# Three large PSUM tiles, fp32r transposes behind a DMA copy, and projections chained to a stream

## The chip, the cores and the metric

One NeuronCore of a Trainium2 chip runs the whole program. Its engines are TensorE (PE in the profile, with PEld for its weight loads), VectorE (DVE), ScalarE (ACT), GpSimd (POOL) and SyncE (SP), which issues most DMAs. The metric is the device time of one execution in microseconds; lower is better.

## The reference

One encoder layer is applied to two groups with the same weights, a prompt of 1024 tokens and a sample of 512, in fp32. Its core:

```python
h = rms_norm(x, ln_pre)
z = h @ w_in                  # pool_in, pool_gate, q, k, v, attn_gate, xq, x_gate, merge_logits
pool_out = multiscale_pool(pool_in, w_pool, pool_scale)
q = apply_rope(rms_norm(q, q_norm), cos, sin);  k = apply_rope(rms_norm(k, k_norm), cos, sin)
attn_out = self_attention(q, k, v)              # softmax(q k^T) v, 8 heads of 64, 2 k/v heads
cross_out = cross_attention(xq, rms_norm(mem, ln_mem), w_mem_kv)   # 4 heads of 128, 256 memories
branches = (pool_out * silu(pool_gate), attn_out * silu(attn_gate), cross_out * silu(x_gate))
gates = sigmoid(merge_logits + b_merge)
merged = sum over n of gates[n] * (branches[n] @ w_branch[n])
return x + rms_norm(merged @ w_out, ln_post)
```

The model width is 1024, the input projection has 6400 columns, and everything is kept to fp32 accuracy.

## The kernel before

Matrices are multiplied in fp32r, a form of fp32 that the matmul takes in one pass. Each operand is split into a high part (a copy rounded to fp32r on ACT, `split`, L165) and a low part (the rest, on DVE, L162), and `mm3` (L126 through `mm`) adds high x high, high x low and low x high in PSUM. A transpose is a matmul with an identity: `tr` (L130) uses `ident` for fp32 tiles and `identr` for fp32r tiles.

PSUM is shared out in two kinds of tiles. `A()` is 128 x 1024 (two banks), and there are two of them; `B()` is 128 x 512 (one bank), and there are four. A tile's next user waits until the last reader of its earlier user is done. A scheduler orders the instructions of each engine by priority and puts in the waits; what an engine then does is fixed.

The program runs in these stages:

- the memories' keys and values (`mem_phase`), and the prompt group's normalised input (`long_h`);
- `products`, the prompt group's input projection. Two weight tiles of 128 columns and the two token blocks of 512 make a 2 x 2 block product, done with seven products in place of eight (25 pairs of weight tiles). The seven products accumulate in banks named by the letters of "XYXZXZX", each product being twelve matmuls of 512 columns. Some results are read between: `keep` (L358, ACT) copies a partial sum out, `summed` (L416, DVE, or L414, ACT) adds a kept one to a bank. Tails of finished projections (`kv_tail`, `q_tail`, `pool_tail`) come in between as background;
- `plain`, the sample group's projections: 24 matmuls for each weight tile into one B tile. Nine pairs are run by themselves, the other pairs become the fill of the next stage;
- the stream. Its units are 64 self-attention units of the prompt (`attention`), 8 cross-attention units (`cross`), 16 double units of the sample (`pairs_of`) and 4 cross units. A unit has four steps: `ahead` loads, `scores` computes scores into an A tile, the row maximum (L782 for the first 64) and the exponential (L784), whose probabilities POOL scales (L786); `turn` transposes them, eight 128 x 128 pieces into an A tile, and splits the result; `values` multiplies with v into a B tile and gates. `stream` runs, in iteration i, scores of unit i, turn of unit i - LAG and values of unit i - LAG - VLAG, and after each step `weave` lets as much of the fill run as the step's share allows;
- what is left of the fill, and then `branches(0)`: branch outputs are loaded from DRAM, split (L165), multiplied with `w_branch` into B tiles and merged with the gates (L996, L998);
- three `block` stages with the other branch projections, the output projection (`out_phase`, in A and B tiles), the norm and the stores.

Intermediate results (q, gates, branch outputs) go through scratch in DRAM, loaded and stored by SP.

## Time and profile before

| | us |
|---|---|
| median of 3 runs | 1500.23 |
| lowest run | 1493.72 |
| the profiled execution's own time | 1496.65 |
| span of that profile, first to last instruction | 1494.8 |
| PE busy | 1456.0 (97%) |
| DVE busy | 976.5 (65%) |
| ACT busy | 709.6 (47%) |
| POOL busy | 273.3 (18%) |
| DMA queue 1, share of 16 engines | 42.7% |

One of the three runs took 2429.65 us; the median leaves it out. In the profile's rows "out<-in" are tiles without their numbers, "xN" is how many instructions a row stands for, and what follows "<-" in brackets or behind a time is the instruction that ended a wait. Matmuls overlap, so their lengths (0.39 us for 512 columns) are longer than the step from one start to the next (0.23 us).

### The profile page before, as it was taken

The numbers are of one execution on the slowest core, as the hardware profiler recorded it, in microseconds if no ns is written. First come the engines' busy times: TensorE is split into PE (matmuls) and PEld (weight loads), VectorE is DVE, ScalarE is ACT, GpSimd is POOL, SyncE is SP. The second block draws the span as 40 slices with busy tenths as digits, with TensorE's granted clock in tenths as the row PEclk, the third lists the DMA queues.
The fourth block names the chain that finished last, engine by engine and source line by source line (L and its number), as shares of the span: only waits on it lengthen the run. The fifth ranks groups of instructions, "written<-read, shape, count | busy, mean of one in ns | idle before, by whom it ended". The sixth has DMA issues, their size and how long they took to land.

```text
span 1494.8 us, 19564 instructions
## 1 busy us (share of the span) xinstructions
PE 1456.0 (97%) x7264; PEld 1210.1 (81%) x7264; DVE 976.5 (65%) x1215; ACT 709.6 (47%) x1083; POOL 273.3 (18%) x286
## 2 busy tenths in 40 slices
PE   7979999999999999999999999999998999999998
PEld 5768888888888888887888888888886888888887
DVE  6996586666648564747767666676775664764764
ACT  6444444544434545434656556566675233323332
POOL 1000020110000000301222222234232150250241
PEclk9989999999999999999999999999999999999999
DMA  7513233332422434344222223165446844954952
GB/s 277 172 47 106 85 114 125 108 132 66 129 92 78 158 133 128 102 150 148 64 96 80 91 68 106 58 219 173 155 155 214 286 148 132 347 193 140 336 163 84
DMA packets 88174, 211.37 MB, mean 141 GB/s; under 512 B 9872, under 2 KB 19216, under 8 KB 87312
## 3 DMA queue, kind: packets, MB, share of 16 engines
q1 hardware_dynamic: 88080, 210.14, 42.7%
q8 instruction: 57, 0.93, 0.3%
q14 instruction: 37, 0.30, 0.1%
HBM read 155.57 MB, written 54.53 MB: 141 GB/s over the span
## 4 chain that ended last, share of the span: by engine, by line
PE 85%; DMA 4%; DVE 4%; ACT 4%; issue 2%; SPq 1%; POOL 0%; DVEq 0%; POOLq 0%; ACTq 0%
PE B L126 66%; PE A L126 14%; PE A L130 5%; ACT u L784 1%; DVE s L782 1%; ACT whi L165 1%; DMA raw<-wt 1%; DVE wlo L162 1%; PE B L130 1%; DMA hu<-xq 1%; ACT med L165 1%; SPq L139 1%; DMA u<-x_prompt 0%; DMA hu<-merge 0%; DMA hu<-x_gate 0%
## 5 line engine op out<-in xcount | busy, mean ns | idle before, releaser
L126 PE MATMUL B<-med,whi 128*128 128x512 f32 x2776 | 871.2, 394 | 15.8 <-ACT med L165 15.8
L126 PEld LDWEIGHTS B<-med,whi 128*128 128x128 f32 x2776 | 515.8, 189 | 122.2 <-ACT med L165 17.5
L126 PE MATMUL B<-med,wlo 128*128 128x512 f32 x1388 | 544.1, 392 | 0.6 <-DVE wlo L162 0.6
L126 PEld LDWEIGHTS B<-med,wlo 128*128 128x128 f32 x1388 | 261.9, 189 | 56.6 <-DVE wlo L162 1.7
L162 DVE TENSOR_TENSOR wlo<-raw,whi 128x1024 fp32r<-128x1024 f32 (+1 forms) x169 | 213.3, 1263 | 141.6 <-ACT whi L165 140.7
L165 ACT ACTIVATE whi<-raw 128x1024 fp32r<-128x1024 f32 (+1 forms) x169 | 167.5, 991 | 288.5 <-PE B L126 198.3
L165 ACT ACTIVATE med<-A 128x1024 fp32r<-128x1024 f32 x92 | 94.3, 1025 | 108.4 <-PE A L130 108.2
L162 DVE TENSOR_TENSOR med<-A,med 128x1024 fp32r<-128x1024 f32 (+1 forms) x93 | 113.0, 1215 | 42.0 <-ACT med L165 40.8
L187 POOL TENSOR_SCALAR s<-s 128x16 f32<-128x16 f32 (+3 forms) x17 | 6.9, 404 | 669.0 <-DVE s L556 333.2
L786 POOL TENSOR_SCALAR u<-u,s 128x1024 f32<-128x1024 f32 x64 | 72.1, 1127 | 251.3 <-DVE s L785 219.1
L130 PE MATMUL A<-ident,u 128*128 128x128 f32 x784 | 102.8, 273 | 0.9 <-DVE med L162 0.2
L130 PEld LDWEIGHTS A<-ident,u 128*128 128x128 f32 x784 | 90.1, 140 | 16.3 <-issue 5.2
L998 POOL TENSOR_TENSOR med<-med,hu 128x512 f32<-128x512 f32 x48 | 77.0, 1617 | 142.3 <-DVE hu L996 142.2
L782 DVE TENSOR_REDUCE s<-A 128x1 f32<-128x1024 f32 x64 | 78.1, 1220 | 32.9 <-PE A L126 11.3
L126 PE MATMUL A<-kt,med 128*128 128x512 f32 x320 | 91.9, 409 | 2.7 <-ACT u L784 1.2
L126 PE MATMUL A<-whi,med 128*128 128x512 f32 (+1 forms) x320 | 92.4, 368 | 0.2 <-ACT hu L1027 0.2
L784 ACT ACTIVATE u<-A,s 128x1024 f32<-128x1024 f32 x64 | 71.3, 1114 | 38.4 <-DVE s L782 38.0
L165 ACT ACTIVATE whi<-sum 128x1024 fp32r<-128x1024 f32 x50 | 53.1, 1062 | 65.6 <-PE B L126 63.7
L162 DVE TENSOR_TENSOR med<-med,med 128x1024 fp32r<-128x1024 f32 (+1 forms) x50 | 55.8, 1127 | 38.1 <-ACT med L165 34.2
L165 ACT ACTIVATE med<-med 128x1024 fp32r<-128x1024 f32 (+1 forms) x44 | 44.2, 1017 | 74.8 <-POOL med L998 36.2
L162 DVE TENSOR_TENSOR wlo<-sum,whi 128x1024 fp32r<-128x1024 f32 x50 | 61.1, 1221 | 23.3 <-ACT whi L165 22.4
L126 PE MATMUL B<-med,vt 128*128 128x256 f32 x512 | 75.9, 287 | 0.4 <-ACT med L165 0.4
(179 smaller groups left out, 1610.4 us busy)
## 6 DMA issues: line engine op xcount, KB each, us to landing
raw<-wt SPq DMA_DIRECT2D x168, 512.0 KB, 3.7
merge<-hu SPq DMA_DIRECT2D x72, 256.0 KB, 2.0
hu<-merge SPq DMA_DIRECT2D x72, 256.0 KB, 5.2
med<-br SPq DMA_DIRECT2D x36, 256.0 KB, 5.6
q<-hu SPq DMA_DIRECT2D x24, 256.0 KB, 2.6
br<-hu SPq DMA_DIRECT2D x24, 256.0 KB, 2.3
med<-q SPq DMA_DIRECT2D x12, 512.0 KB, 5.0
med<-xt_prompt SPq DMA_DIRECT2D x4, 1024.0 KB, 13.2
```

What stands on the lines that cost most here:

```text
L126: pe.matmul(out, l, r, **k)
L130: pe.transpose(out, x, i[:])
L139: return nc.sync.dma_start(out, src)
L162: v.tensor_tensor(out, x, hi.bitcast(F32), op=ALU.subtract)
L165: act.activation(hi, x, AF.Copy)
L187: pool.tensor_scalar(ss, ss, EPS, 1.0, op0=ALU.add, op1=ALU.mult)
L782: v.reduce_max(mx[:], a[:], axis=AX.X, negate=True)
L784: act.activation(p, a[:], AF.Exp, bias=mx[:], accum_out=sm[:])
L786: pool.tensor_scalar(p, p, rc[:], 1.0, op0=ALU.mult, op1=ALU.mult)
L998: pool.tensor_tensor(at, at, sg[:], op=ALU.add)
```

## The change

- There are three A tiles and two B tiles, eight banks as before.
- In `products` the banks X and Z become the two halves of one A tile, Y stays a B tile. `plain` takes its tile from a function: the nine pairs that run alone use the halves of an A tile (`halves`), the fill uses B tiles (`single`).
- The units get a fifth step, `hand_on`: one iteration after the scores, a DMA issued by ACT copies the scaled probabilities, 512 KB, into another tile of the same pool, declared fp32r (`handed`, L776 in the new file). `turn` transposes that copy with `identr` into an A tile declared fp32r. LAG goes from 2 to 3.
- Stores of finished branch outputs are collected in `finished` and issued at the end of the next iteration.
- `branches(0)` is chained to the fill, and in the iterations after the last unit the fill's share is doubled.
- `long_h` copies the spread factors from the B tile into SBUF.

```diff
     def A(dt=F32):
-        return ps.tile([P, 1024], dt, tag="A", bufs=2, name=nm("A"))
+        return ps.tile([P, 1024], dt, tag="A", bufs=3, name=nm("A"))
     def B(dt=F32):
-        return ps.tile([P, 512], dt, tag="B", bufs=4, name=nm("B"))
+        return ps.tile([P, 512], dt, tag="B", bufs=2, name=nm("B"))
...
             for i, bank in enumerate("XYXZXZX"):
                 ready(p * 4 + i // 2 + LOOK)
                 start = bank not in banks
-                if start:
-                    banks[bank] = B()
-                b = banks[bank][:, :n]
+                if bank == "Y":
+                    banks[bank] = B()[:, :n]
+                elif not banks:
+                    a = A()
+                    banks["X"] = a[:, :n]
+                elif start:
+                    banks[bank] = a[:, BLK:BLK + n]
+                b = banks[bank]
...
+    def single(i):
+        return B()
+    def halves():
+        a = []
+        def bank(i):
+            if i == 0:
+                a[:] = [A()]
+            return a[0][:, i * BLK:(i + 1) * BLK]
+        return bank
...
+    def handed(p):
+        t = U(F32R)
+        act.dma_start(t.bitcast(F32), p)
+        return t
+    def hand_on(state):
+        def hand(i):
+            state[i] = handed(state[i])
+        return hand
...
-            tp = A()
+            tp = A(F32R)
             for c in range(nch):
-                tr(tp[:, c * P:(c + 1) * P], p[:, c * P:(c + 1) * P], ident)
+                tr(tp[:, c * P:(c + 1) * P], p[:, c * P:(c + 1) * P], identr)
...
         for i in range(-2, n + LAG + VLAG):
-            more = units[min(max(i, 0), n - 1)][5] * SHARE / 3
-            for k, lag in enumerate((-2, 0, LAG, LAG + VLAG)):
+            more = units[min(max(i, 0), n - 1)][6] * SHARE / 3 * (1 + (i >= n))
+            late = finished[:]
+            finished.clear()
+            for k, lag in enumerate((-2, 0, LAG, LAG + VLAG, 1)):
                 if 0 <= i - lag < n:
-                    units[i - lag][k](units[i - lag][4])
-                if k > 0 and i >= 0:
+                    units[i - lag][k](units[i - lag][5])
+                if 0 < k < 4 and i >= 0:
                     yield more
+            for out, x in late:
+                nc.sync.dma_start(out, x)
...
-    run(plain(pairs[0], hs, bg))
+    run(plain(pairs[0], hs, bg, halves()))
...
+    fill = chain(fill, branches(0, sc, merged))
     weave(stream(units), fill)
     run(fill)
-    run(branches(0, sc, merged))
...
-LAG, VLAG, SHARE, LOOK, WAIT = 2, 2, 0.66, 1, 6
+LAG, VLAG, SHARE, LOOK, WAIT = 3, 2, 0.66, 1, 6
```

**First piece of order.** PE's instructions in one pair of merge gates of `products`. Before, B_3056 is bank X and B_3122 bank Z; the rows are the last matmul of a product and the first of the next, with what that waits for:

```order
L126 MATMUL B_3122<-med_514,whi_3104 128x512 x2
L126 MATMUL B_3122<-med_514,wlo_3105 128x512
L126 MATMUL B_3056<-med_517,whi_3137 128x512 [waits Activation_49]
...
L126 MATMUL B_3056<-med_520,wlo_3138 128x512
L126 MATMUL B_3122<-med_523,whi_3137 128x512 [waits Activation_49]
...
L126 MATMUL B_3122<-med_526,wlo_3138 128x512
L126 MATMUL B_3056<-med_531,whi_3171 128x512 [waits DVE_49]
```

Now, where A_3045 holds X in its first half and Z in its second:

```order
L126 MATMUL A_3045<-med_518,wlo_3094 128x512
L126 MATMUL A_3045<-med_521,whi_3125 128x512 [waits Activation_49]
...
L126 MATMUL A_3045<-med_524,wlo_3126 128x512
L126 MATMUL A_3045<-med_527,whi_3125 128x512 [waits DVE_49]
...
L126 MATMUL A_3045<-med_530,wlo_3126 128x512
L126 MATMUL A_3045<-med_535,whi_3159 128x512 [waits DVE_49]
```

The products stand in the same order, but the waits have moved. Followed to the instruction that fulfils them, the three waits before are for reads of the product before the last: the copies of products 3 and 4 and the sum with product 5, each out of the same bank that is written next. Now each wait is for the read of the product that has just ended, out of the tile's other half: the copy of product 4, the sum with product 5, and the sum with product 6.

**Second piece of order.** ACT's instructions in the stream, among the self-attention units. Before (`u` are probabilities, L784 the exponential, L165 with `med<-A` the copy of transposed probabilities):

```order
L165 ACTIVATE med_6623<-A_6673 128x8x128 [waits PE_49]
L784 ACTIVATE u_6669,s_6666<-A_6660,s_6665 128x1024 [waits DVE_49,Pool_49]
L882 ACTIVATE hu_6605<-B_6651 64x256 [waits PE_49]
L784 ACTIVATE u_6705,s_6702<-A_6696,s_6701 128x1024 [waits DVE_49,Pool_49]
L165 ACTIVATE med_6728<-A_6730 128x8x128 [waits PE_49]
L165 ACTIVATE med_6728<-A_6763 128x8x128 [waits PE_49]
L784 ACTIVATE u_6759,s_6756<-A_6750,s_6755 128x1024 [waits DVE_49,Pool_49]
```

Now, with L776 the copy for the next step, L813 the exponential and L911 the copy that was L882:

```order
L911 ACTIVATE hu_6451<-B_6501 64x256 [waits PE_49]
L813 ACTIVATE u_6521,s_6518<-A_6512,s_6517 128x1024 [waits DMAHW7_49,DVE_49,Activation_49]
L776 DMA u_6547<-u_6467 128x1024 [waits DMAHW5_49,Pool_49]
L813 ACTIVATE u_6558,s_6555<-A_6549,s_6554 128x1024 [waits DMAHW1_49,DVE_49,Activation_49]
L165 ACTIVATE med_6581<-A_6583 128x8x128 [waits PE_49]
L776 DMA u_6603<-u_6521 128x1024 [waits Pool_49]
L813 ACTIVATE u_6615,s_6612<-A_6606,s_6611 128x1024 [waits DMAHW2_49,DVE_49,Activation_49]
L165 ACTIVATE med_6581<-A_6619 128x8x128 [waits PE_49]
```

Between exponentials there now stand DMA issues that wait for POOL (the scaling of the probabilities), each one or two exponentials behind the one whose result it copies.

More of the change, by code (lines that the diff above doesn't have):

```diff
@@ L249, in long_h @@
             yield
-            sp.append(spread(rj))
+            sp.append(HU())
+            spread(rj, sp[j][:])
             yield
@@ L391, in products, with plain @@
                 yield
-    def plain(pairs, h, background):
+    def plain(pairs, h, background, bank):
         for k0, k1, take in pairs:
             for i, key in enumerate((k0, k1)):
-                w, b = weights(*key), B()
+                w, b = weights(*key), bank(i)
                 for k in range(KC):
@@ L816, in values @@
             gated(state, jp, hd, o, gd, out, b)
-        return [(ahead, scores, turn, values, i, 2560) for i in range(len(units))]
+        return [(ahead, scores, turn, values, hand_on(state), i, 2560) for i in range(len(units))]
     def pairs_of(sc, kt, vt):
@@ L870, in values @@
             gated(state, jp, hd, o, gd, out, 0)
-        return [(ahead, scores, turn, values, i, 2560) for i in range(len(units))]
+        return [(ahead, scores, turn, values, hand_on(state), i, 2560) for i in range(len(units))]
     def gated(state, jp, hd, o, gd, out, b):
@@ L939, in turn @@
             p = state[c]
-            tp = A()
+            tp = A(F32R)
             for m in range(2):
                 for t in range(TT):
-                    tr(tp[:, m * 512 + t * P:m * 512 + (t + 1) * P], p[:, t * 256 + m * P:t * 256 + (m + 1) * P], ident)
+                    tr(tp[:, m * 512 + t * P:m * 512 + (t + 1) * P], p[:, t * 256 + m * P:t * 256 + (m + 1) * P], identr)
             pt = M()
-            split(pt[:, 0:1024], pt[:, 1024:2048], tp[:])
+            split(pt[:, 0:1024], pt[:, 1024:2048], tp[:].bitcast(F32))
             state[c] = pt
@@ L957, in values @@
                 v.tensor_tensor(g[:], o[:], g[:], op=ALU.mult)
-            nc.sync.dma_start(out[c][:, bs], g[:])
-        return [(ahead, scores, turn, values, c, 3410) for c in range(NXH)]
+            finished.append((out[c][:, bs], g[:]))
+        return [(ahead, scores, turn, values, hand_on(state), c, 3410) for c in range(NXH)]
     def branch_parts(field, bs):
@@ L1103, in encoder_kernel @@
     scs, kts, vts, pairs, bg, _, drained = group(0)
-    run(plain(pairs[0], hs, bg))
+    run(plain(pairs[0], hs, bg, halves()))
     merged = []
-    fill = drained(plain(pairs[1], hs, bg))
+    fill = drained(plain(pairs[1], hs, bg, single))
     units = [u for b in range(2) for u in attention(b, sc, kt, vt)]
```

15 lines of the change are left out of this document (9 added, 6 removed).

## The prediction

> **What bounds the kernel now.** I read the page's busy times and chain first, then the stages in windows, then single waits.
>
> ```profile
> PE 1456.0 (97%) x7264; PEld 1210.1 (81%) x7264; DVE 976.5 (65%) x1215; ACT 709.6 (47%) x1083; POOL 273.3 (18%) x286
> PE 85%; DMA 4%; DVE 4%; ACT 4%; issue 2%; SPq 1%; POOL 0%; DVEq 0%; POOLq 0%; ACTq 0%
> 104.00:593.00 489.00, 488.83 (x2230) 403.04 (x2229) 312.84 (x416) 219.12 (x311) 29.07 (x28) 1.00 0.35 112
> 687.00:1149.00 462.00, 456.52 (x2697) 386.92 (x2695) 316.19 (x391) 289.11 (x507) 139.77 (x168) 1.00 0.38 122
> 1149.00:1162.00 13.00, 6.34 (x15) 4.50 (x16) 4.09 (x5) 2.11 (x2) 0.00 (x0) 0.61 0.96 334
> ```
>
> PE (TensorE) is 97% busy and 85% of the chain that ends last. The window rows (length; busy time of PE, weight loads, DVE, ACT, POOL; granted clock; DMA share; GB/s) say the same by stage: 104 to 593 us is the seven-product loop (`products`), where PE never rests and DVE and ACT are busy 64% and 45%; 687 to 1149 is the attention stream with its fill; 1149 to 1162 is the border to the branch projections, where PE stands and its clock falls to 0.61. So what the change makes PE do, or wait for, goes into the time one for one. That holds most strictly in the loop, which has no slack to give.
>
> **The change part by part.** *Transposes.* Rows of PE's timeline are start, length, instruction and count:
>
> ```profile
> 748.98 1.08 PE L126 MATMUL A<-kt,med 128*128 128x512 f32 x4
> 749.90 1.04 PE L130 MATMUL A<-ident,u 128*128 128x128 f32 x8
> 750.69 1.19 PE L126 MATMUL B<-med,vt 128*128 128x256 f32 x8
> 751.72 0.40 PE L126 MATMUL B<-med,whi 128*128 128x512 f32 x1
> 118.39 0.45 PE L130 MATMUL B<-identr,u 128*128 128x128 f32 x4
> 118.67 0.70 PE L126 MATMUL B<-med,whi 128*128 128x512 f32 x2
> ```
>
> From start to next start, eight fp32 transposes take 0.79 us (749.90 to 750.69) and four fp32r ones 0.28, so eight would take 0.56. Each of the 92 units (64 + 12 + 16) has eight: 92 x 0.23 = 21 us less PE work. The ends are 0 (the new tiles behave like fp32) and 21.
>
> *A third A tile, one more unit of lag.* The window over the 64 scores' maxima (L782), and who held back the scores' weight loads:
>
> ```profile
> 895.90:953.68 57.78, 14.60 (x12) 1.00 0.27 87
> L126 PEld LDWEIGHTS A<-kt,med 128*128 128x128 f32 x320 | 55.5, 188 | 24.3 <-ACT u L784 10.9 <-DVE med L162 1.8 <-DMA med<-q 1.3
> ```
>
> Twelve units took 57.78 us, 4.82 each. A unit needs 0.92 + 0.79 + 1.03 us by the rows above, and a third of 24 fill matmuls at 0.23 (the step from 392.26 to 392.49 below), 1.8: together 4.6. So up to 0.25 us of a unit is waiting for an A tile that the exponential still reads; over 64 units 16 at most, 0 at least. I take -9.
>
> *Hand-on copies.* 92 new DMAs of 512 KB, issued from ACT's queue, which waits there for POOL's scaling; behind each stand an exponential and the copies that empty PSUM, and PE waits for those.
>
> ```profile
> 744.58 0.32 SPq L471 DMA_DIRECT2D x_gate<-hu  x1
> raw<-wt SPq DMA_DIRECT2D x168, 512.0 KB, 3.7
> med<-q SPq DMA_DIRECT2D x12, 512.0 KB, 5.0
> u<-x_prompt SPq DMA_DIRECT2D x8, 512.0 KB, 6.5
> L784 ACT ACTIVATE u<-A,s 128x1024 f32<-128x1024 f32 x64 | 71.3, 1114 | 38.4 <-DVE s L782 38.0
> ```
>
> An issue holds SP's queue 0.32 us; 92 of them add 29 us to ACT's 289 in 462, so ACT stays under 70%. The copy's own time is hidden by the longer lag, if it lands in time. In the second piece of order shown above, the copy u_6547 stands behind the exponential u_6521. From those scores to the transposes of u_6547, PE has two groups of transposes, values and scores and twelve fill matmuls: 2 x (0.56 + 1.03 + 0.92) + 2.7 = 7.7 us. The maximum (14.60 over 12, 1.22), the exponential (1.11, its sum read 0.2) and the hops take 2.7. So 5.0 us remain for the copy, and that is the place with the least room, one unit in three. At 3.7 (the weights' row) nothing waits, at 5.0 almost nothing, at 6.5 31 units wait 1.5. I take 3.7 to 5.0, since the DMA share there is 0.38 and the copy adds about as much again: +3 us, from 0 to +15. Stores that move one unit later are issued by SP, which waits for nobody that PE needs: 0.
>
> *Branch projections in the fill.* What stands at the border now:
>
> ```profile
> 1154.51 1.06 ACT L165 ACTIVATE med<-med 128x1024 fp32r<-128x1024 f32 x1 [9.00 <-DMA med<-br]
> 1155.62 2.06 PE L126 MATMUL B<-med,whi 128*128 128x512 f32 x3 [7.05 <-ACT med L165]
> ```
>
> PE stands 7.05 us until the branch input is loaded and split, and the low clock after it costs some 3 more. With the projections chained to the fill their loads start earlier. But the order then puts the last three groups of transposes, each behind its exponential, its scaling and now a 3.7 us copy, ahead of the first projection. I give back about half: -4 us, from -10 to 0.
>
> *X and Z as halves of one A tile.* This is the term that decides. In the first piece of order, the group into Z waits for the copy (L359, L358 before) or sum (L434, L416 before) that reads X's result, and the other way round. In the kernel before, these were separate tiles and the wait was for the group before the last. So before, twelve matmuls covered each read; now nothing does. The same pair of merge gates in the trace of before:
>
> ```profile
> L331 DVE TENSOR_TENSOR sum<-raw 128x512 f32<-128x512 f32 x25 | 17.3, 690 | 16.5 <-DMA raw<-wt 16.2
> 392.26 0.39 PE L126 MATMUL B<-med,wlo 128*128 128x512 f32 x1
> 392.49 0.39 PE L126 MATMUL B<-med,whi 128*128 128x512 f32 x1
> 392.74 0.60 ACT L358 ACTIVATE hu<-B 128x512 f32<-128x512 f32 x1 [1.32 <-issue]
> 394.98 0.39 PE L126 MATMUL B<-med,wlo 128*128 128x512 f32 x1
> 395.21 0.39 PE L126 MATMUL B<-med,whi 128*128 128x512 f32 x1
> 395.77 0.58 ACT L358 ACTIVATE hu<-B 128x512 f32<-128x512 f32 x1
> 397.70 0.39 PE L126 MATMUL B<-med,wlo 128*128 128x512 f32 x1
> 397.93 0.39 PE L126 MATMUL B<-med,whi 128*128 128x512 f32 x1
> 398.20 0.69 DVE L416 TENSOR_TENSOR hu<-B,hu 128x512 f32<-128x512 f32 x1 [1.61 <-PE B L126]
> 400.42 0.39 PE L126 MATMUL B<-med,wlo 128*128 128x512 f32 x1
> 400.65 0.39 PE L126 MATMUL B<-med,whi 128*128 128x512 f32 x1
> 400.85 0.69 DVE L416 TENSOR_TENSOR hu<-B,hu 128x512 f32<-128x512 f32 x1 [1.96 <-PE B L126]
> ```
>
> Products 3, 4, 5 and 6 of a pair each end with the first row of a triple; the next product starts 0.23 us later, and only then is the result read. In the new order it starts when that read has ended, and 0.05 us after it:
>
> ```profile
> 466.79 0.58 ACT L358 ACTIVATE hu<-B 128x512 f32<-128x512 f32 x1
> 467.42 0.30 PEld L126 LDWEIGHTS B<-med,whi 128*128 128x128 f32 x2 [0.32 <-ACT hu L358]
> 467.42 0.73 PE L126 MATMUL B<-med,whi 128*128 128x512 f32 x2
> 468.00 0.39 PE L126 MATMUL B<-med,wlo 128*128 128x512 f32 x1
> ```
>
> Here a wait of this kind ended at 467.37 and PE went on at 467.42; its weights had to be loaded first, so the two matmuls took 0.58 to the next start where two take 0.45: 0.13 more. For the pair above: 393.39 - 392.49 = 0.90; 396.40 - 395.21 = 1.19; 398.94 - 397.93 = 1.01; 401.59 - 400.65 = 0.94. The sum is 4.04, with 4 x 0.13 4.56 us a pair, and there are 25 pairs (L331): 114. The scheduler has put other matmuls or transposes into some of these places; by the built order 63 of the 100 have none and all together hold 17 us of PE work. So **+97 us**. The low end has every read start 0.43 us after the last matmul starts (as at 400.42 to 400.85) and no reload: 2 x 0.84 + 2 x 0.95 = 3.6 a pair, 90 - 17 = +73. The high end has all four like the worst, 1.19 + 0.13: 132 - 17 = +115. What lies behind PE there (weight splits, tails) only gets more time.
>
> By the Trainium skill (PSUM — Partial Sum Buffer, Summary: rules for kernel authors), one reads PSUM while a matmul runs by sending the matmul to another bank. X and Z are such halves, so by that rule the wait isn't needed and this term would be 0 (rival 1). The built order has the wait all the same, and an engine obeys its program.
>
> *The sample group's first projections* use the same halves, nine times with one wait, and a few weight splits come out just ahead of their matmuls: +6, from 0 to +12.
>
> The two B tiles left cost nothing that I can see: in the stream and the later blocks a B tile comes round after two groups, 2.7 us or more, and its read takes 1.0 to 1.2 as above.
>
> Sum: -21 - 9 + 3 - 4 + 97 + 6 = +72 us. Against the profiled execution's own 1496.65 us (span 1494.8 and 1.85 around it) that is **1569 us**. The median shown, 1500.23, is 0.2% above that execution, the fastest, 1493.72, 0.2% below it. The ends together: 73 - 21 - 16 - 10 = +26 (1523) and 115 + 15 + 12 = +142 less 0 to 21 for the transposes (1618 to 1639).
>
> **The rivals.** (1) *Faster:* the loop's waits cost next to nothing, because each read is over before PE has drained. It ends with the gains alone, -21 - 9 + 3 - 4 = -31: 1466 us. For it speaks that the stage is built to be covered, against it that the fastest read above ends 0.94 us late. Under 0.3 us a wait (31 over 100) the change gains; only near 0 is it over 2%. Chance 0.04. (2) *Within the noise:* everything at its good end, 1523 us, 0.09. (3) *The copies come late:* DMA contention makes them 6.5 us as for x_prompt, 31 units wait 1.5 us, 46 more: 1615 us. The DMA share of 0.38 speaks against it, its doubling for it; 0.07. (4) *The clock falls:* in the border row above it went down in a gap of 7 us, while at 687 to 1149, with waits below 1.6 us, it stayed 1.00. If waits of 1 us after every 2.7 us drew it down to 0.75 on average, the loop's 489 us became 652: 1569 + 163 = 1732 us, 0.03. The Trainium skill (TensorE: Matmul & The Clock Gate, A second HAM failure mode: psum-queue depth-cycling) tells of just that: short idle times between groups of matmuls, often enough, let the clock swing between half and full. The stream's rows don't show it, and no run here has waits this dense. That the fp32r transposes take as long as fp32 ones is part of my range (1590).
>
> **How the numbers follow.** My forecast, 1569, has 0.77. Its own range is 1530 to 1615. A measurement of this kernel can tell about 2%, 30 us, from no change: 1467 to 1527. Faster by more is rival 1, 0.04; the same is rival 2, 0.09; slower is the rest, 0.87. The range from 1528 to 1615 leaves out rival 1, most of rival 2, half of 3 and all of 4, some 0.2.
>
> **What would show it.** In the profile after, the loop's stage should be 80 to 115 us longer, with PE's idle time ended by ACT L359 and DVE L434 in some 100 places of 0.8 to 1.3 us; transposes A<-identr should start 0.07 us apart; the stream should be 25 to 35 us shorter, with L776 issues landing in 4 to 5 us. I am wrong if L359 and L434 end no idle time of PE, or if the transposes wait for L776.

## The result, and the profile after

The changed kernel takes 1617.57 us (median of four runs, 1613.56 to 1620.03) where the kernel before takes 1498.28 (median of four): a ratio of 1.0805, 95% interval 1.0764 to 1.0845. The slow run of 2429.65 us counts in that median and in the one shown before, but not in the ratio. The forecast was 1569, so it was too low by 49 us. Its range ended at 1615, though the ends that it had added up reached 1639. The profiled execution took 1617.73 us.

Two lines of the page after:

```profile
PE 1472.0 (91%) x7264; PEld 1198.2 (74%) x7264; DVE 972.9 (60%) x1215; ACT 711.5 (44%) x1085; POOL 271.6 (17%) x286
PE 20%; DMA 3%; DVE 2%; issue 1%; ACT 1%; POOL 0%; SPq 0%; DVEq 0%; ACTq 0%; POOLq 0%
```

And the windows over its stages (columns as in the prediction; the last number but two is the granted clock):

```profile
72.00:665.00 593.00, 516.60 (x2233) 399.17 (x2232) 339.02 (x440) 229.17 (x322) 26.93 (x28) 0.99 0.28 90
665.00:802.00 137.00, 123.14 (x550) 97.52 (x551) 65.69 (x99) 46.37 (x70) 14.66 (x13) 0.98 0.38 117
802.00:1347.00 545.00, 520.01 (x3059) 444.31 (x3058) 359.53 (x443) 314.63 (x531) 166.90 (x184) 0.98 0.64 226
1347.00:1615.00 268.00, 251.22 (x1162) 208.79 (x1161) 153.06 (x161) 82.69 (x119) 57.50 (x49) 0.97 0.57 190
```

PE's busy time hardly grew (1456.0 to 1472.0), but its share fell from 97% to 91%: the kernel now waits. The chain's shares add up to 27%, since it is lost on its way back; it can't be read as before, so the stages have to carry the comparison. Their borders are the first and last copy of a product's result, the first score, and the first reading of the output projection, in the kernel before and after (count, shortest/median/longest ns, first and last start):

```profile
L358 ACT ACTIVATE hu<-B x75: 577/598/602, 72.2 to 574.4; 128x512 f32<-128x512 f32 x75
...
L126 PE MATMUL A<-kt,med x320: 387/394/506, 692.4 to 1113.2; 128*128 128x512 f32 x160
...
L1026 DVE TENSOR_TENSOR med<-A,u x20: 418/684/693, 1243.5 to 1481.2; 128x512 f32<-128x512 f32 x16, 128x256 f32<-128x256 f32 x4
```

```profile
L359 ACT ACTIVATE hu<-A x75: 578/597/603, 72.1 to 664.7; 128x512 f32<-128x512 f32 x75
...
L126 PE MATMUL A<-kt,med x320: 387/396/628, 802.1 to 1207.8; 128*128 128x512 f32 x160
...
L1063 DVE TENSOR_TENSOR med<-A,u x20: 417/688/692, 1346.6 to 1601.7; 128x512 f32<-128x512 f32 x16, 128x256 f32<-128x256 f32 x4
```

| stage | before | after | difference | predicted |
|---|---|---|---|---|
| loop (first to last copy) | 502.2 | 592.5 | +90 | +97 |
| first projections of the sample (to the first score) | 118.0 | 137.5 | +19.5 | +6 |
| stream and first branch projections (to the first reading in `out_phase`) | 551.1 | 544.4 | -7 | -31 |
| the rest (to the end) | 251.4 | 269.1 | +18 | 0 |

So the loop is as forecast. The missing 49 us lie in the other three stages: 13.5, 24 and 18, less 7 in the loop. PE's waits name the same places (releaser; us in all, times, longest):

```profile
PE A L126 <- ACT hu L359: 32.8, 40, 1.3
PE A L126 <- DVE hu L434: 23.6, 32, 0.9
...
PE A L130 <- DMA u<-u: 16.6, 8, 7.3
PE B L126 <- DVE med L1033: 8.1, 3, 3.9
PE A L126 <- DVE u L434: 7.2, 9, 0.9
PE A L126 <- ACT med L432: 6.7, 3, 4.5
...
PE A L130 <- ACT whi L165: 2.9, 1, 2.9
```

The last row is a wait for a copy too: it ends 0.14 us after the landing of a copy issued at 1232.8, as the other eight end 0.13 to 0.14 us after theirs. So PE waits 19.5 us for copies, in nine places.

*The loop.* From the timeline of one pair:

```profile
432.81 0.39 PE L126 MATMUL A<-med,wlo 128*128 128x512 f32 x1
...
433.24 0.69 DVE L434 TENSOR_TENSOR hu<-A,hu 128x512 f32<-128x512 f32 x1 [3.10 <-PE A L126]
...
433.99 0.73 PE L126 MATMUL A<-med,whi 128*128 128x512 f32 x2 [0.78 <-DVE hu L434]
...
434.56 0.40 PE L126 MATMUL A<-med,wlo 128*128 128x512 f32 x1
```

The last matmul of a product starts at 432.81, its sum is read from 433.24 to 433.93, and only then, at 433.99, does the next product start, in the other half of the tile. That is 1.18 us where 0.23 was the step, and the next two matmuls take 0.57 in place of 0.45: 0.95 and 0.12 us, close to the 0.94 and 0.13 of the prediction's working. The rows above count 81 such waits (40, 32 and 9) where some 100 were forecast; 78 of them lie in the loop, and at 1.07 us each they make, by this estimate, 83 of its 90 us.

*The first projections.* Their longest wait:

```profile
697.69 0.69 DVE L582 TENSOR_TENSOR med<-med,s 128x512 f32<-128x512 f32 x1
698.41 0.63 ACT L600 ACTIVATE med<-med 128x512 fp32r<-128x512 f32 x1 [2.42 <-DVE med L582]
698.95 0.58 ACT L432 ACTIVATE med<-A 128x512 f32<-128x512 f32 x1
...
699.58 0.73 PE L126 MATMUL A<-med,whi 128*128 128x512 f32 x2 [4.51 <-ACT med L432]
```

The copy L432 that frees the half is short, but it stands on ACT behind L600, which waits for a row of VectorE's work on the keys. In the kernel before, with a B tile for each result, PE has no wait in this stage. Here its waits add up to 14.9 us, and behind two of them (from 700.3 and from 744.7) the granted clock is 0.50 for 3.4 us each, some 3 us more.

*The stream.* One late copy:

```profile
1002.02 0.89 SPq L139 DMA_DIRECT2D med<-q  x2
...
1003.24 0.47 ACTq L776 DMA_DIRECT2D u<-u  x1
...
1008.55 1.11 PE L126 MATMUL A<-kt,med 128*128 128x512 f32 x4
...
1012.39 0.85 PE L130 MATMUL A<-identr,u 128*128 128x128 f32 x8 [2.73 <-DMA u<-u]
```

All copies, from issue to landing:

```profile
DMA to landing us min/median/max: 2.9/3.4/10.0
```

And the time that eight transposes take, from start to next start, 0.64 us where it was 0.79:

```profile
816.96 0.80 PE L130 MATMUL A<-identr,u 128*128 128x128 f32 x8
...
817.60 0.46 PE L126 MATMUL B<-med,whi 128*128 128x512 f32 x1
```

The usual copy lands in 3.4 us, better than forecast. This one was issued 1.2 us after two loads of q and took 9.0. Eleven of the 92 took over 6 us, and each of these shared its time with a load of q, of the memory's keys and values (1 MB each), or of the branch inputs. On the good side, the waits for the exponential are gone from the scores' weight loads (they were 10.9 of 24.3 us idle before):

```profile
L126 PEld LDWEIGHTS A<-kt,med 128*128 128x128 f32 x320 | 56.7, 189 | 9.9 <-DVE med L162 0.3
```

*The rest.* A place behind the first output projection:

```profile
1376.07 0.39 PE L126 MATMUL B<-med,wlo 128*128 128x512 f32 x1
...
1377.14 2.48 DVE L1057 SCALAR_TENSOR_TENSOR u<-med,s,u 128x1024 f32<-128x1024 f32 x2 [1.10 <-POOL s L191]
1379.54 1.28 DVE L1033 SCALAR_TENSOR_TENSOR med<-hu,B 128x512 f32<-128x512 f32 x2
...
1380.37 1.19 PE L126 MATMUL B<-med,whi 128*128 128x512 f32 x2 [3.91 <-DVE med L1033]
...
1381.78 1.06 PE L126 MATMUL B<-med,whi 128*128 128x512 f32 x2
```

VectorE waits for POOL, does two passes of the norm's end (L1057), and only then reads the two branch projections (L1033) that PE has finished. With four B tiles PE had two more to write into; with two it stands 3.9 us, and the granted clock is 0.50 from 1379.6 to 1386.4 (two matmuls in 1.06 us where 0.62 is usual). In this stage the waits for L1033 are 10.4 us; three stretches at half clock, 13.6 us together, cost some 6 more. That is about 17 of the 18 us.

### The profile page after: what moved, and what is told of

Same layout as the page of the kernel before. It is cut to its first block, busy times and chain, and to the rows that moved or that the text cites. A ratio compares the mean times of both kernels' runs of the same rounds, so it can differ in the third digit from the quotient of the medians.

```text
span 1615.7 us, 19657 instructions
## 1 busy us (share of the span) xinstructions
PE 1472.0 (91%) x7264; PEld 1198.2 (74%) x7264; DVE 972.9 (60%) x1215; ACT 711.5 (44%) x1085; POOL 271.6 (17%) x286
## 5 line engine op out<-in xcount | busy, mean ns | idle before, releaser
L126 PE MATMUL A<-med,whi 128*128 128x512 f32 x1488 | 477.3, 402 | 86.6 <-ACT hu L359 32.8
L126 PE MATMUL B<-med,whi 128*128 128x512 f32 x1288 | 409.1, 398 | 16.0 <-DVE med L1033 8.1
L126 PEld LDWEIGHTS A<-med,whi 128*128 128x128 f32 x1488 | 272.3, 189 | 178.8 <-ACT hu L359 50.5
L165 ACT ACTIVATE whi<-raw 128x1024 fp32r<-128x1024 f32 (+1 forms) x169 | 167.1, 990 | 382.5 <-PE A L126 219.7
L126 PEld LDWEIGHTS B<-med,whi 128*128 128x128 f32 x1288 | 241.8, 191 | 70.6 <-issue 15.1
L126 PE MATMUL A<-med,wlo 128*128 128x512 f32 x744 | 291.0, 393 | 0.0
L126 PE MATMUL B<-med,wlo 128*128 128x512 f32 x644 | 254.7, 395 | 0.0
L126 PEld LDWEIGHTS A<-med,wlo 128*128 128x128 f32 x744 | 140.8, 189 | 31.2 <-DVE wlo L162 0.2
L126 PEld LDWEIGHTS B<-med,wlo 128*128 128x128 f32 x644 | 122.7, 191 | 26.1
L165 ACT ACTIVATE med<-A 128x1024 fp32r<-128x1024 f32 x92 | 94.4, 1026 | 66.1 <-PE A L130 65.5
L130 PEld LDWEIGHTS A<-identr,u 128*128 128x128 f32 x736 | 72.4, 141 | 33.3 <-issue 14.7
L165 ACT ACTIVATE whi<-sum 128x1024 fp32r<-128x1024 f32 x50 | 53.1, 1062 | 96.7 <-PE A L126 55.6
L130 PE MATMUL A<-identr,u 128*128 128x128 f32 x736 | 75.5, 246 | 19.5 <-DMA u<-u 16.6
L813 ACT ACTIVATE u<-A,s 128x1024 f32<-128x1024 f32 x64 | 71.4, 1115 | 39.6 <-issue 26.2
```

Of the source, the lines that this page charges most:

```text
L126: pe.matmul(out, l, r, **k)
L130: pe.transpose(out, x, i[:])
L165: act.activation(hi, x, AF.Copy)
L813: act.activation(p, a[:], AF.Exp, bias=mx[:], accum_out=sm[:])
```

## The experiments

Theory: the price is the sum of four things that do not touch each other: the halves (loop and first projections), the count of B tiles (rest), the third A tile (a gain in the stream), and copies that land late and so eat what faster transposes give. The rivals are named with each run. All ratios are against the kernel before on the same chip, with 95% intervals. The stages are cut as in the table above.

| kernel | loop | first proj. | stream | rest | median us | ratio |
|---|---|---|---|---|---|---|
| before | 502.2 | 118.0 | 551.1 | 251.4 | 1498.28 | 1 |
| changed | 592.5 | 137.5 | 544.4 | 269.1 | 1617.57 | 1.0805 (1.0764-1.0845) |
| e1 X, Z apart | 500.5 | 117.9 | 543.2 | 266.1 | 1506.24 | 1.0083 (1.0065-1.0101) |
| e2 PSUM tiles alone | 592.3 | 137.4 | 542.3 | 268.4 | 1613.30 | 1.0799 (1.0780-1.0818) |
| e3 PSUM tiles of before | 499.7 | 117.4 | 550.8 | 252.2 | 1495.51 | 1.0005 (0.9994-1.0016) |
| e4 no copies | 592.5 | 135.1 | 542.9 | 266.0 | 1615.38 | 1.0804 (1.0779-1.0830) |
| e5 e1, merges in A and B | 499.8 | 117.4 | 545.3 | 251.3 | 1489.62 | 0.9965 (0.9949-0.9981) |
| e6 e5, no copies | 500.2 | 118.0 | 540.1 | 251.0 | 1483.83 | 0.9936 (0.9921-0.9951) |
| e7 e5, fp32r without copies | 501.0 | 117.9 | 524.3 | 250.9 | 1466.47 | 0.9814 (0.9799-0.9828) |
| e8 e5, spread | 500.5 | 118.0 | 540.9 | 251.5 | 1485.80 | 0.9947 (0.9929-0.9965) |
| e9 e5, more traffic | 500.2 | 118.4 | 541.0 | 251.6 | 1489.03 | 0.9965 (0.9952-0.9979) |
| e10 e5, lag 4 | 500.7 | 118.2 | 535.2 | 251.8 | 1475.60 | 0.9869 (0.9852-0.9885) |
| e11 e6, unchained | 500.7 | 117.5 | 536.0 | 251.3 | 1476.33 | 0.9883 (0.9868-0.9898) |
| e12 before, new tiles | 500.7 | 117.6 | 539.1 | 251.1 | 1483.02 | 0.9924 (0.9909-0.9939) |
| e13 e5, 77 copies | 500.4 | 117.5 | 526.8 | 251.4 | 1469.86 | 0.9832 (0.9816-0.9848) |
| e14 e10, unchained | 500.8 | 117.6 | 530.0 | 251.3 | 1472.57 | 0.9850 (0.9833-0.9868) |
| e15 e14, no copies | 500.6 | 117.8 | 537.1 | 251.3 | 1480.78 | 0.9903 (0.9887-0.9920) |
| e16 e11, stores early | 499.7 | 118.0 | 535.9 | 251.6 | 1477.20 | 0.9874 (0.9852-0.9896) |
| e17 e13, unchained | 501.3 | 117.8 | 527.9 | 252.0 | 1468.89 | 0.9830 (0.9814-0.9847) |

**The change taken apart: e1 to e4.** The edit of e1, to the changed kernel:

```diff
-                elif not banks:
-                    a = A()
-                    banks["X"] = a[:, :n]
                 elif start:
-                    banks[bank] = a[:, BLK:BLK + n]
+                    banks[bank] = A()[:, :n]
...
-            if i == 0:
-                a[:] = [A()]
-            return a[0][:, i * BLK:(i + 1) * BLK]
+            return A()[:, :BLK]
```

> The changed kernel, but X and Z of every pair in the seven-product loop, and the two results of a pair in the sample group's first projections, each get an A tile of their own. Theory (the read of one half holds up the write of the other): the loop loses its some 90 waits on L359 and L434 and is back at about 512 us from 68 us on, where the changed kernel takes 605; the first projections go from 129 to about 115. The kernel takes 1617 - 93 - 14 = 1510 us. Rival (PE waits there because only two B tiles or three A tiles are left, whoever shares them): the loop stays above 580 us and the kernel above 1590.

Measured 1506.24. The loop is at 500.5 and the first projections at 117.9, with three A and two B tiles still:

```profile
L359 ACT ACTIVATE hu<-A x75: 577/598/605, 72.1 to 572.6; 128x512 f32<-128x512 f32 x75
```

In these two stages the sharing of a tile was the price, not the number of tiles. e2 goes the other way, with the change's tiles alone on the kernel before:

```diff
-        return ps.tile([P, 1024], dt, tag="A", bufs=2, name=nm("A"))
+        return ps.tile([P, 1024], dt, tag="A", bufs=3, name=nm("A"))
-        return ps.tile([P, 512], dt, tag="B", bufs=4, name=nm("B"))
+        return ps.tile([P, 512], dt, tag="B", bufs=2, name=nm("B"))
...  (and X and Z, and the nine pairs of plain, as halves)
```

> The kernel before with the change's PSUM tiles alone: three A, two B, X and Z as halves, the sample group's first projections as halves; no copies, fp32 transposes, lag 2, no chained branches, stores as before. Theory (beside the loop's 93 us, the first projections cost 17 and the two B tiles 18 in the blocks behind the stream, where the trace after shows PE waiting 3.9 us and more on L1033): 1498 + 93 + 17 + 18 - 10 for the third A tile = 1616 us, as slow as the whole change. Rival (the two B tiles cost nothing, as predicted, and what went beyond the prediction is the copies): 1498 + 97 + 6 - 9 = 1592 us.

Measured 1613.30: the tiles alone are the whole change's price within 4 us, stage by stage, also in the stream (542.3). So whatever else was changed comes to nothing in sum. e3 is the opposite kernel, with everything else and the old tiles:

```diff
-        return ps.tile([P, 1024], dt, tag="A", bufs=3, name=nm("A"))
+        return ps.tile([P, 1024], dt, tag="A", bufs=2, name=nm("A"))
-        return ps.tile([P, 512], dt, tag="B", bufs=2, name=nm("B"))
+        return ps.tile([P, 512], dt, tag="B", bufs=4, name=nm("B"))
...  (and X, Z and the nine pairs in B tiles)
```

> The changed kernel with the PSUM tiles of before: two A, four B, X, Y and Z in B tiles, the first projections too; copies, fp32r transposes, lag 3, chained branches and later stores stay. Theory (transposes give 30, late copies take 18 of it and another 7 at the stream's end, and with two A tiles their gain is missing): 1498 - 30 + 25 = about 1493 us, from 1485 to 1500. Rival (the prediction's terms: transposes -21, copies +3, border -4): 1476 us.

Measured 1495.51, the same as before within 0.2%. The prediction's terms would have given 1476. And e4:

```diff
-            tp = A(F32R)
+            tp = A()
-                tr(tp[:, c * P:(c + 1) * P], p[:, c * P:(c + 1) * P], identr)
+                tr(tp[:, c * P:(c + 1) * P], p[:, c * P:(c + 1) * P], ident)
...
-        return [(ahead, scores, turn, values, hand_on(state), i, 2560) for i in range(len(units))]
+        return [(ahead, scores, turn, values, lambda _: None, i, 2560) for i in range(len(units))]
```

> The changed kernel without the hand-on copies: the probabilities stay in their tile and are transposed as fp32; the rest of the change stays, the lag of three units too. Theory (the copies' late landings cost nearly what the faster transposes give): 1617 + 30 - 25 = about 1622 us, within 10 us of the changed kernel, with PE's waits for the copies gone (16.6 us in eight places) and the transposes 30 us longer. Rival (the prediction's terms, +21 - 3): 1636 us.

Measured 1615.38, and the ratio is that of the changed kernel. Copies with faster transposes are worth nothing here.

**The B tiles: e5.**

```diff
-            pj = B()
+            pj = (A() if d % 2 else B())[:, :BLK]
```

> The kernel of e1 (X and Z in A tiles of their own), and the branch projections' results alternate between a B and an A tile. Theory (with two B tiles PE runs out of results to write into while VectorE still has two of L1057's passes ahead of L1033): the stretch behind the stream's first 24 merges, 283.8 us in e1 and 267.9 before, is back at 267 to 270 and the kernel at 1506 - 16 = 1490 us. Rival (the waits on L1033 come from the later loads of the merge gates, not from the count of tiles): no change, 1506 us.

Measured 1489.62; the rest is at 251.3, as before the change. A third tile to write into is enough; nothing was done to the loads of the gates, so the rival falls.

**What the transposes give and the copies take: e6 and e7.** e6 does to e5 what e4 does to the changed kernel; e7 has exponential and scaling write fp32r at once, and so leaves out the low halves of the probabilities:

```diff
-                p = U()
+                p = U(F32R)
-            pool.tensor_scalar(p, p, rc[:], 1.0, op0=ALU.mult, op1=ALU.mult)
+            pool.tensor_scalar(p, p.bitcast(F32), rc[:], 1.0, op0=ALU.mult, op1=ALU.mult)
...  (and no hand_on)
```

> As e5, without the hand-on copies and with fp32 transposes. Theory: as between the changed kernel and e4, faster transposes (92 groups of eight, 0.79 against 0.64 us, 14 us) and late copies cancel: 1488 us, within 6 us of e5. Rival (in e4 the loop hid a difference): e5 is faster by 10 us or more.

> As e5, without the copies, but with fp32r transposes: exponential and scaling write the probabilities as fp32r, so their low halves are left out; the work of every engine but the copies stays. Theory: the transposes give their 14 us whole against e6, about 1474 us, and no wait for a copy is left; 15 to 17 us below e5. Rival (the copies' waits only show time that PE would lose elsewhere in the stream, to ScalarE or VectorE): within 5 us of e5.

Measured 1483.83 and 1466.47. From e6 to e7 only the transposes change: 15.8 us less in the stream (540.1 to 524.3). From e7 to e5 only the copies come in: 21.0 us more (545.3). So the copies cost 5 us more than the transposes give. The time without copies was not lost again to ScalarE or VectorE, so e7's rival falls. Of e5's waits these two rows bear on it:

```profile
PE A L130 <- DMA u<-u: 11.9, 7, 2.8
PE B L126 <- ACT med L165: 10.7, 1, 10.7
```

Two more waits, of 2.4 and 0.3 us, end 0.14 us after a copy's landing though their rows name VectorE: 14.5 us in nine places. The second row, the wait for the branch input at the stream's end, is 6.9 us in e7.

**Why the copies land late: e8, e9, e10, e13.** Two of these edits did not do what they were meant to. e8 issued the loads of q one unit apart in the code, and left out the last two copies:

```diff
-            if hd == 0 and j == 0:
-                t = M()
-                for x in range(2):
-                    load(t[:, x * D:(x + 1) * D].bitcast(F32), qd[b * TT + jp * 2 + x][:])
-                state["q", jp] = t
+            if hd == 0:
+                if j == 0:
+                    state["q", jp] = M()
+                load(state["q", jp][:, j * D:(j + 1) * D].bitcast(F32), qd[b * TT + jp * 2 + j][:])
...
-                for k, src in (("mk", mkd), ("mv", mvd)):
+                for k, src in ((("mk", mkd), ("mv", mvd))[c],):
```

> As e5, but the loads that are on their way when the copies land late are spread: the two 512 KB loads of q one unit apart, the memory's values one unit behind its keys; and the sample group's last two cross units are transposed as fp32 without a copy. Theory (a copy lands late because it shares the DMA engines with these loads): the copies' longest landing falls from 10 us to some 7, PE's waits for u from 14 to 17 us to under 5, the kernel takes 1490 - 10 = 1480 us. Rival (the copies are late by their own queue, whatever else is loaded): the waits stay above 10 us and the time within 4 us of e5.

Measured 1485.80, but the loads of q were still issued 0.4 us apart (745.81 and 746.23, for one), and so were the memory's (964.46 and 964.94): both loads of a pair waited for the same tile to come free. The longest landing stayed 9.5 us and the waits 13.9. The 4 us are within the spread (the intervals of e5 and e8 overlap); if they are real, they fit the stream's end, where PE's wait for the branch input fell from 10.7 to 5.5 us. On the loads the run tells nothing. e9:

```diff
                     load(t[:, x * D:(x + 1) * D].bitcast(F32), qd[b * TT + jp * 2 + x][:])
+                    load(spare[x][:], qd[b * TT + jp * 2 + x][:])
```

> As e5, and beside each of the prompt group's loads of q (two of 512 KB, at 683, 743, 817 and 889 us in e5) the same bytes are also copied from memory to memory. Theory (a copy lands late because it shares the DMA engines with such a load): PE's three waits for u behind the loads at 743, 817 and 889, 1.5, 1.1 and 2.7 us in e5, grow to 4 to 8 us each, and the kernel takes 1490 + 12 = 1502 us, from 1497 to 1510. Rival (the copies are late by their own queue or by ScalarE's issue): the waits and the time stay as in e5, 1490 us.

Measured 1489.03, as e5. The added copies wait for no tile, so they were issued at 282 to 326 us, in the loop, and met nothing. The run tells only that 4 MB of traffic in the loop are free. e10 gives the copies more time:

```diff
-LAG, VLAG, SHARE, LOOK, WAIT = 3, 2, 0.66, 1, 6
+LAG, VLAG, SHARE, LOOK, WAIT = 4, 2, 0.66, 1, 6
```

> As e5, with a lag of four units between scores and transposes in place of three. Theory (one more unit, 4.6 us, covers a late landing): the waits for u inside the stream, some 8 us without its end, are gone and the kernel takes 1490 - 8 = 1482 us. Rival (a copy holds its U tile one unit longer and seven are too few, so that exponentials or copies wait for a tile): the stream gets longer, 1495 us or more.

Measured 1475.60: 14 us gained where 8 were expected. No wait for a copy is left in it, and the seven U tiles are enough. By the trace e5's waits for copies are 14.5 us in all; the expectation had counted 8, without the stream's end. e13 leaves out only the late ones:

```diff
     def hand_on(state, first):
         def hand(i):
-            state[i] = handed(state[i])
+            if first + i not in SKIP:
+                state[i] = handed(state[i])
         return hand
...
+SKIP = {12, 28, 29, 35, 44, 45, 58, 60, 61, 62, 65, 69, 84, 86, 91}
```

(a unit in `SKIP` is transposed with `ident`, as before the change)

> As e5, but 15 of the 92 units are transposed as fp32 without a copy: those whose copies landed late (5.2 to 10 us) in e1, e5, e9 and the changed kernel alike, number 12, 28, 29, 44, 45, 60, 61, 65, 69, 84, 91 and four more, all issued beside loads of q, of the memory's keys and values or of the branch inputs. Theory (only these collide): the longest landing of the others stays under 6.5 us, PE's waits for u fall from 11.9 us to under 3, the kernel takes 1490 - 9 = 1481 us. Rival (the queue itself is late now and then, wherever): other copies take over the lateness, the waits stay above 6 us, the time within 4 us of e5.

Measured 1469.86, 20 us below e5 where 9 were expected: a ratio of 0.983 against the kernel before. The longest landing of the 77 copies that are left, and no row of PE for u at all:

```profile
DMA to landing us min/median/max: 2.9/3.2/6.3
```

The lateness did not move to other copies, so it belongs to those places. That the loads are the reason was not shown by moving a load, since e8 and e9 failed to; the traces speak for it. In the changed kernel 19 of the 92 copies are in flight together with a load of q, of the memory's keys or values, or of a branch input, and all eleven that took over 6 us are among them. Of the other 73 none took more than 5.6 (median 3.2), though in e5 two such copies took 6.9 and 7.0. The loads suffer too: the two of q at 743 us in e5 take 4.6 and 7.8 us, in e6, without copies, 3.7 and 4.6; but those at 889 us take 6.7 and 7.6, in e6 6.5 and 7.3.

e13 gained more than the 14.5 us of waits, and the traces have most of the rest. The wait at the stream's end fell by 4.2 us:

```profile
PE B L126 <- ACT med L165: 6.5, 1, 6.5
```

Two stretches of 3.4 us at a granted clock of 0.50, which in e5 come right behind waits for copies (at 753.2 and 900.0 us), are gone, some 3 us. The 15 units that are transposed as fp32 give back 15 x 0.15 us. Together that is an estimate of 20 us, where the stream got 18.5 shorter.

**Chaining, lag and stores: e11, e12, e14 to e17.** e11 undoes the chaining in e6:

```diff
-    fill = chain(fill, branches(0, sc, merged))
     weave(stream(units), fill)
     run(fill)
+    run(branches(0, sc, merged))
...
-            more = units[min(max(i, 0), n - 1)][6] * SHARE / 3 * (1 + (i >= n))
+            more = units[min(max(i, 0), n - 1)][6] * SHARE / 3
```

> As e6 (no copies), but the first branch projections come behind the stream's fill again, as in the kernel before. Theory (in e6 PE stands 7.1 us for the split of a branch input, as long as the 7.05 us before the change, so chaining gained nothing): within 4 us of e6, 1480 to 1488. Rival (the prediction's term): 4 to 10 us slower, 1488 to 1494.

Measured 1476.33: 7.5 us faster without the chaining, which neither side had expected. The waits of PE for the split of the branch input, in e6 and in e11:

```profile
PE B L126 <- ACT med L165: 7.1, 1, 7.1
```

```profile
PE B L126 <- ACT med L165: 2.4, 1, 2.4
```

In e6 the first branch projection stands in PE's order ahead of the stream's last values, so these wait with it; unchained they run while the branch input is loaded. e12 puts the three A tiles into the kernel before, without the halves and with e5's merges:

```diff
                 if start:
-                    banks[bank] = B()
-                b = banks[bank][:, :n]
+                    banks[bank] = (B if bank == "Y" else A)()[:, :n]
+                b = banks[bank]
...
+        return lambda i: A()[:, :BLK]
...
-            pj = B()
+            pj = (A() if d % 2 else B())[:, :BLK]
```

> The kernel before with three A and two B tiles, X and Z and the sample group's first projections in A tiles of their own, and branch projections that alternate between A and B; no lag, copies, chained branches or later stores. Theory (all of e6's gain is the third A tile, as in the stretch from the first scores to the 24th merge: 534.6 us before, 524 in e2, e4 and e6): 1494 - 10 = 1484 us. Rival (the longer lag or the chaining has a share in it): 1488 us or more.

Measured 1483.02: the stream falls from 551.1 to 539.1 by the new tiles alone, without lag or copies. That it is the third A tile among them is read from the scores' weight loads, which no longer wait for the exponential:

```profile
L126 PEld LDWEIGHTS A<-kt,med 128*128 128x128 f32 x320 | 56.2, 188 | 10.1 <-DMA med<-q 1.0
```

e14 undoes the chaining where there are copies and lag 4 (e11's edit on e10):

> As e10 (copies, lag 4), with the first branch projections behind the stream's fill as in the kernel before. Theory (the chained projections stand ahead of the stream's last units in PE's order and wait 13.2 us for their inputs in e10): 7 to 10 us below e10, 1467 us. Rival (chaining cost only where there are no copies): within 3 us of e10, 1476 us.

Measured 1472.57, 3 us below e10 (ratios 0.9850 and 0.9869, whose intervals overlap): if the difference is real, it has e11's sign and less than half its size. In e14 PE waits for a copy at the stream's end again (3.2 us). e15 takes the copies out of e14 (e4's edit):

> As e14, without copies and with fp32 transposes. Theory (with lag 4 the copies land in time, so that the faster transposes keep their 14 us): 1467 + 12 = 1479 us, and about the 1476 of e11, whose lag of three is enough without copies. Rival (lag 4 gives e10 its gain by itself): within 4 us of e14.

Measured 1480.78. With enough cover the copies now leave 8 us of the transposes' gain, not the 12 expected, and lag 4 without copies gives nothing over lag 3 (1476.33 in e11). e16 puts the stores of e11 back:

```diff
-            finished.append((out[c][:, cs], ot[:, :256]))
+            nc.sync.dma_start(out[c][:, cs], ot[:, :256])
...
-            finished.append((out[c][:, bs], g[:]))
+            nc.sync.dma_start(out[c][:, bs], g[:])
```

> As e11 (no copies, lag 3, not chained), with the stores issued as in the kernel before. It differs from e12 by the lag alone. Theory (stores cost nothing wherever they stand): 1476 us as e11, and the lag of three gives the 7 us over e12. Rival (the later stores give them): 1482 us or more.

Measured 1477.20, as e11: the later stores are worth nothing, and the lag of three some 3 us by the stream's length (539.1 to 535.9), 6 by the medians. Last, e17 undoes the chaining in e13:

> As e13 (15 of 92 units without a copy), with the first branch projections behind the stream's fill as in the kernel before. Theory (PE's 6.5 us for the split of the branch input at the stream's end go as in e11 and e14, 3 to 7 us): 1465 us, from 1462 to 1467. Rival (in e13 the shorter stream has taken that room already): within 2 us of e13's 1470.

Measured 1468.89: within 1 us of e13. Here the chaining costs nothing that can be measured. e13 and e17 are the two fastest kernels here that leave nothing out, 1.7% below the kernel before.

## Why the prediction was wrong, and where it was right

The sum was 49 us too low. The copies and the two B tiles were each 18 us dearer than forecast, the first projections 13.5, the border 8 and the transposes 5; the loop was 7 cheaper, and the third A tile with the lag gave 6 more. The terms of the stream and of the B tiles are measured in kernels without the halves (e5 and later), not in the changed kernel itself.

**Right: the halves.** The loop's +97 measured +90, inside its 73 to 115, and e1 shows the cause. There X, Y and Z are read and written side by side: during each of the 75 copies L359 a matmul starts, in the changed kernel during 35 of them, and the loop takes 500.5 us. The Trainium skill's rule (PSUM — Partial Sum Buffer, Summary: rules for kernel authors), that PSUM may be read while a matmul writes to another bank, agrees with e1. The wait came from the program, which orders by whole tiles, not from the memory. Rival 1 fell with it.

**Right in the loop: the clock.** From 86 to 700 us, with some 80 waits of 0.8 us, the granted clock (the last number but two) stayed 1.00, so rival 4 fell. Behind longer waits it dropped, and for that the sum had a term at the border alone:

```profile
86.00:700.00 614.00, 537.96 (x2336) 416.19 (x2336) 338.46 (x445) 232.69 (x328) 29.42 (x31) 1.00 0.28 92
867.60:871.00 3.40, 3.40 (x11) 2.72 (x11) 2.43 (x3) 2.42 (x4) 0.40 (x1) 0.50 0.38 154
1379.60:1386.40 6.80, 6.03 (x14) 4.84 (x15) 2.89 (x5) 0.00 (x0) 0.00 (x0) 0.50 0.92 349
```

The swinging that the Trainium skill tells of (TensorE: Matmul & The Clock Gate, A second HAM failure mode: psum-queue depth-cycling) is not seen with the loop's short waits.

**Right within its range: third A tile and lag** (-9 predicted, at most -16; by the stream's length -12 in e12 and some -3 more in e16) and **the stores** (0; e16).

**Wrong: the hand-on copies, +3, measured +21** (e5 against e7). The step that failed is "I take 3.7 to 5.0, since the DMA share there is 0.38": a mean share and a median landing. The median was indeed 3.4. But the 5.0 us of room is what the latest ones must meet, and eleven of 92 took 6.4 to 10.0, always beside the same kinds of loads. So the transposes did wait for L776, which the prediction had named as a sign of being wrong. Of the 21 us, 14.5 are waits for copies and 3.8 the longer wait at the stream's end. Rival 3 had the likely mechanism, in the wrong shape: it spread 1.5 us over a third of the units, where a few places cost up to 7.3 us each. In the trace the copy from ACT's queue took 9.0 us behind two loads from SP's, where the shortest took 2.9. That agrees with the Trainium skill (DMA: Bandwidth & Descriptors, Issuing engines are not separate DMA queues): DMAs issued from several engines run on the same 16 DMA engines and interleave.

**Wrong in size: the transposes, -21, measured -16** (e6 to e7). The forecast took the far end of its own 0 to 21, and its distance of 0.07 us was read from groups of four into a B tile; in groups of eight it is 0.64 / 8 = 0.08.

**Wrong: the border, -4, measured some +4** (e6 against e11: 3.7 us by the spans, 7.5 by the medians; 0 to 3 in e17 and e14). The prediction saw that a projection drawn forward would stand behind late transposes; it did not ask what stands behind the projection.

**Wrong: the two B tiles, 0, measured +18** (e1 against e5: 15). The step that failed was "a B tile comes round after two groups, 2.7 us or more, and its read takes 1.0 to 1.2 as above". The read itself is that short. But it stands on VectorE behind POOL's step and two passes of L1057, 3.7 us in all (1375.89, where the norm's end begins, to 1379.62), and this happens behind the first two of the three output projections. The two spare tiles were the cover. With the low clock behind these waits, as above, that is nearly all of the 18 us.

**Wrong: the first projections, +6, measured +19.5.** The same mistake on ACT: the nine waits were priced at less than a microsecond each, as if ACT were free when the reads come. Here the reads queue behind other work: 6.7 us of waits are for L432, 4.5 of them in the one place behind the keys' tail (L600). The other 8.2 us are several shorter waits, weight splits among them, and the low clock comes on top.

With the measured terms the stream comes to -12 - 3 - 16 + 21 + 4 = -6 (-7 in its stage), and all to +90 + 19.5 + 18 - 6 = +121.5, against +121 between the two profiled spans.

## What to carry to other kernels

Halves of one PSUM tile are one tile to whatever orders the program: give two results that are read in turn two tiles. The number of tiles that a fast engine needs is set not by how long a read takes but by the longest row of work that may stand ahead of that read on its engine; look for that row before taking tiles away. A DMA that stands in a short loop must be priced by its slowest landing beside the other loads, and where only a few are late, leave it out just there: that took the kernel from 0.35% below the one before (e5) to 1.7% (e13). And a wait costs more than its length where the clock drops behind it.

## What the runs showed of the hardware that was not expected

- The eleven copies that took over 6 us in the changed kernel are the same eleven that did in e1, up to 9.3 us. With a lag of four units (e10) others are late as well.
- The issue of one of these 512 KB copies holds ACT's queue 0.47 us (median of 92); on SP's queue the issue of a weight load of the same size takes 0.33, of a load of q 0.43.
- fp32r transposes of 128 x 128 start 0.079 us apart on average in groups of eight (fp32: 0.109), and 0.070 in groups of four.
- The stretches at a granted clock of 0.50 last 3.4 us or a multiple of it (6.8, 10.2, 13.7). The length of a single wait does not decide whether one follows: in the changed kernel one does behind a wait of 1.6 us (at 866.1), and none behind one of 2.7 (at 1012.4). What decides it no run here shows.
